# A two-layer decoder trunk in split float32: one 256-column product for the norms' factors, and byte distances between the operands of each product stage

## The chip, the core and the metric

The kernel runs on one core of a Trainium2 chip. The metric is the device time of one execution in microseconds (us). Before the change three runs gave 594.59, 595.46 and 595.98 us; their median is 595.46 us. Beside these runs there is one profiled execution, from which every row of a trace in this document comes.

## The reference

256 tokens of width 1024 pass through two layers. Layer A has differential attention over 256 tokens, layer B has block-sparse attention, which for 256 tokens is one causal block. Both layers also attend into a fixed memory of 256 rows, and both end in a squared-ReLU MLP of width 4096.

```python
h = _rmsnorm(x, a_norm_attn[i]);  z = h @ a_w_in[i]              # 1024 x 2560
o_self = _diff_attention(q, k, v, lam, lam_init, a_subln[i])
o_mem = _memory_attention(qm, mem, a_mem_norm[i], a_w_mem_kv[i])
x = x + jnp.concatenate([o_self, o_mem], axis=-1) @ a_w_out[i]   # 1024 x 1024
u = jax.nn.relu(_rmsnorm(x, a_norm_mlp[i]) @ a_w_up[i])          # 1024 x 4096
x = x + (u * u) @ a_w_down[i]                                    # 4096 x 1024
...
hk = _rmsnorm(x, kv_norm);  kv = hk @ w_kv                       # 1024 x 1536
h = _rmsnorm(x, b_norm_attn[j]);  z = h @ b_w_in[j]              # 1024 x 1024
...
return _rmsnorm(x, final_norm)
```

## The kernel before

**Split products.** Every large product is made from three products in float32r: each operand is split into a high part (h: the value cast to float32r, by ScalarE) and a low part (l: the remainder, by VectorE), and TensorE adds h·h, h·l and l·h into one PSUM bank. Weights arrive in 192 chunks of 128 x 1024 float32 (buffers `w`), are cast into `wh` (L336) and their remainders into `wl` (L338). Names of a row read `out<-moving,stationary`: the first operand streams through the array, the second was loaded into it (PEld) beforehand, while the matmul ahead of it ran.

**The product stages,** in the order of a layer:

- `nat_block` (L497): the attention's input products. The tokens are stationary (128 columns), 512 columns of weights move. Which token tile is used depends on the call: `xn` in layer A and for keys and values in layer B, `B2`/`B3` (printed as `B`) for queries in layer B, weight buffers for the memory.
- `out_proj` (L763): weights stationary, 256 tokens of the tile pair `B0`/`B1` (the attention's output `O`) move.
- `up_chunk` (L819): weights stationary, 256 tokens of `xn` move. The first 256-column result can be used once the norms' factors are known.
- `natural_down` (L869): the tokens' activations u (`B0` to `B7`) stationary, 512 columns of weights move. For six pairs of chunks (`FAST`, `fast_pair`) seven block products take the place of eight; four of the seven have sums of blocks of u as stationary operand. These sums are split into `xn` as well (L918 on ScalarE, L919 on VectorE), two of its eight slots for each pair, four pairs before a slot is used again.

**The norms' factors.** Gains go into the tokens ahead of a product and the factor 1/rms behind it. For the MLP, `Stats.rstd` (L458) sums squares on TensorE, VectorE computes the two columns of factors (128 tokens each), and `bcast` (L475 to L479) spreads them over all partitions: two diagonal matrices of 128 x 128 on VectorE, two plain float32 products with a matrix of ones on TensorE, which the trace shows as four passes, and a copy into `rb`.

**Order.** `Plan` orders all steps by a planner with costs and priorities and emits one stream for each engine; a step waits for the last writer of what it reads and for all readers of what it overwrites, by the keys it names. Tiles of the pool `const` lie one behind the other in the order of their first use, then those of the pool `ring`; a tile starts at a multiple of 32 bytes.

**Distances.** For what follows, the distance of two successive matmuls is the byte address (within a partition) of the second one's stationary operand less that of the first one's moving operand, modulo 512; 512 bytes are the 128 float32 columns of a stationary operand. All `w`, `wh`, `wl` and `B` buffers start 416 bytes past a multiple of 512, `xn` starts 352 past one, and every step within them is a multiple of 512. So the distance is 0 in L763, in L869 with u and in L497 with `B` or the memory; 448 in L497 and L869 with `xn` as stationary operand; and 64 in L819, where `xn` moves.

Of the kernel before, what the change touches and what calls it, by code (L numbers as in the profile page):

```python
# [9 lines left out]
F32 = mybir.dt.float32  # L10
F32R = mybir.dt.float32r
# [3 lines left out]
OP = mybir.AluOpType  # L15
AX = mybir.AxisListType

D, S, FF = 1024, 256, 4096
KT = D // 128
# [5 lines left out]
HELD = 6  # L25
FAST = (1, 3, 5, 7, 9, 11)
CW = 1024

# [182 lines left out]
def t_dve(n, scalar=False):  # L213
    return 69 + 1.041 * n + (61 if scalar else 0)
# [11 lines left out]
def tile_hybrid(ctx: ExitStack, tc: tile.TileContext, xa, xb, memt, xnat, mnat, w0, wall, consts, fgain, out):  # L226
    nc = tc.nc
    const = ctx.enter_context(tc.tile_pool(name="const", bufs=1))
# [11 lines left out]
    def name(s):  # L240
        uid[0] += 1
        return f"{s}_{uid[0]}"

    def buf(cls, shape, dt=F32, pool=None):
        pool = pool or ring
        return Buf(cls, lambda slot: pool.tile(shape, dt, name=name(cls), tag=f"{cls}{slot}", bufs=1))
# [8 lines left out]
    def ppx_buf():  # L255
        return Buf("ppa", lambda slot: ppx[:, slot])

    def fixed(shape, nm, dt=F32):
        return const.tile(shape, dt, name=name(nm))


    NG = len(GAINS) * KT
    xg = fixed([128, NG + KT * S], "xT")
    xT = xg[:, NG:].rearrange("p (k s) -> p k s", k=KT)
    xnt = fixed([128, KT, 2, S], "xn", F32R)
    g = {n: xg[:, i * KT:(i + 1) * KT] for i, n in enumerate(GAINS)}
    cst = fixed([128, 513], "consts")
    trig_t = cst[:, 0:256].rearrange("p (a b e) -> p a b e", a=2, b=2)
# [8 lines left out]
    mv = fixed([128, 2, 4, 64], "mv")  # L277
    vb = fixed([128, 2, 12, 64], "vb")

    wsum = fixed([128, 2048], "wsum")  # L280


# [5 lines left out]
    ones = fixed([128, 128], "ones")  # L288
# [62 lines left out]
    def split_scaled(src, skey, gain, T, k, psrc=False):  # L351
        P.add(("act", t_act(S, psrc, True), lambda: nc.scalar.activation(T.h(k), src(), AF.Copy, scale=gain)),  # L352
              skey, [T.hk(k)])
        P.add(("dve", t_dve(S, True), lambda: nc.vector.scalar_tensor_tensor(  # L354
            T.l(k), src(), gain, T.h(k).bitcast(F32), op0=OP.mult, op1=OP.subtract)),
            list(skey) + [T.hk(k)], [T.lk(k)], port=not psrc)

    xn = Tiles(lambda k: xnt[:, k, 0], lambda k: xnt[:, k, 1], lambda k: ("xnh", k), lambda k: ("xnl", k))

    def big(i, shape, dt=F32):  # L360
        return buf(f"B{i}", shape, dt)

    def big_tiles(i, j):
        h, l = big(i, [128, KT, S], F32R), big(j, [128, KT, S], F32R)
        return Tiles(lambda k: h.t[:, k], lambda k: l.t[:, k], lambda k: (h, k), lambda k: (l, k))

    @early("prep")
    def norm_tile(gname, T, k):
# [101 lines left out]
    def bcast(st):  # L470

        ps = bank("t")
        for h in range(2):
            dg = buf("dg", [128, 128])
            P.add(("dve", 196, lambda dg=dg, h=h: nc.vector.tensor_scalar_mul(dg.t, ident, st.r[:, h:h + 1])),  # L475
                  [st.key], [dg])
            P.add(("pe", 213, lambda dg=dg, h=h: nc.tensor.matmul(
                ps.t[:, h * 128:(h + 1) * 128], ones, dg.t, start=True, stop=True)), [dg], [ps])
        P.add(("dve", t_dve(S), lambda: nc.vector.tensor_copy(rb_t, ps.t[:, 0:S])), [ps], ["rb"])  # L479


# [367 lines left out]
    def natural_down(us, pss, upto, held, gather, room, rk, depth):  # L849
# [30 lines left out]
        def fast_pair(n, j):  # L880
# [31 lines left out]
            split(3, lambda: t(2, 4), rk(2) + rk(3))  # L912

            q = 2 * (n % depth)
            sh, sl = [xnt[:, q + i].rearrange("p a s -> p (a s)") for i in range(2)]
            kh, kl = [[("xnh", q + i), ("xnl", q + i)] for i in range(2)]
            src, sk = st_["sums"][j]
            P.add(("act", t_act(512), lambda: nc.scalar.copy(sh, src())), sk, kh)  # L918
            P.add(("dve", t_dve(512), lambda: nc.vector.tensor_sub(sl, src(), sh.bitcast(F32))), sk + kh, kl, port=True)  # L919
# [188 lines left out]
    class Mixer:  # L1108


        def __init__(self, diff, rx, qT, kT):
            self.diff, self.rx, self.qT, self.kT = diff, rx, qT, kT
            self.O = big_tiles(0, 1)
            self.vv = big(4, [128, 4, 512]) if diff else None
            st_["pT"] = big(5, [128, 5, 384]) if diff else None
            st_["pp"] = None if diff else big(5, [128, 4, 512])
            st_["p"] = big(6, [128, 4, 512])
            self.zz = big(7, [128, 4, 512])
# [148 lines left out]
    def x_prep(gname, T, st):  # L1267
        def done(m):
            norm_tile(gname, T, m)
            st.add(lambda: xT[:, m], [("x", m)])  # L1270
        return done
# [4 lines left out]
    for k in range(KT):  # L1276
        if k == 0:
            dma(lambda: xg[:, 0:NG + 4 * S], xa, 512 * (NG + 4 * S), w=["g"] + [("x", j) for j in range(4)], pri=-1)
        if k == 4:
            dma(lambda: xg[:, NG + 4 * S:], xb, 512 * 4 * S, w=[("x", j) for j in range(4, 8)], pri=3)  # L1280
        if k % 2 == 0:
            first_ch.append(chunk(2 if k == 0 else 1))
            P.steps[-5].pri = k - 0.5 if k else P.steps[-5].pri
        split_scaled(lambda k=k: xT[:, k], [("x", k), "g"], g["a_norm_attn"][:, k:k + 1], xn, k)
    ra.whole(xnat, 2)
    dma(lambda: cst, consts, 512 * 513, w=["trig", "lam", "sub8"])

# [17 lines left out]
        mem_evac(pss)  # L1305

    ma = Stats()
    mixer_a(Mixer(True, ra, xn, xn), mem_a, x_prep("a_norm_mlp", xn, ma), first_ch)

    st_["layer"] = "B"  # L1310

    rx = Stats()
    xq = big_tiles(2, 3)
    mlp(ma, x_prep("kv_norm", xn, rx))

    def mem_b():
        T = mem_tiles("b_mem_norm")
# [3 lines left out]
        rx.rstd()  # L1321

    mb = Stats()
    mixer_b(Mixer(False, rx, xq, xn), mem_b, x_prep("b_norm_mlp", xn, mb))

    mlp_last(mb)

# [75 lines left out]
```

## Time and profile before

| what | value |
|---|---|
| median of three runs | 595.46 us (594.59 to 595.98) |
| the profiled execution: its own time, and the span of its trace | 598.83 us, 597.1 us |
| mean granted TensorE clock | 0.996 |
| matmul records | 3794 |
| DMA | 108.45 MB, 182 GB/s on average |

All starts and durations below are of the profiled execution, counted from the start of its span. Where a row of the chain says that x matmuls took so many us, the quotient is the time from one matmul's start to the next, which will be called the pitch; the duration of a single record is longer, since matmuls overlap. The same quotient can be formed from two rows of the timeline: the difference of their starts by the matmuls between them.

### The profile page before, as it was taken

How to read it: one execution, taken by the hardware profiler on the slowest of the kernel's cores; microseconds unless marked ns; L12 is line 12 of the kernel's file. 1: busy time of each engine (PE TensorE's matmuls, PEld its weight loads, DVE VectorE, ACT ScalarE, POOL GpSimd, SP SyncE). 2: the span in 40 equal slices, each digit the busy share in tenths (PEclk: the TensorE clock that was granted, in tenths of full speed). 3: DMA queues.
4: the chain of work that ended last, by engine and by line, in shares of the span. 5: the costliest groups of instructions: out<-in, count | busy, mean ns of one | idle time of the engine just before them, and what ended most of it. 6: DMA issues, size and time to landing. Idle time of an engine off the chain costs nothing.

```text
span 597.1 us, 10365 instructions
## 1 busy us (share of the span) xinstructions
PE 586.0 (98%) x3794; PEld 517.7 (87%) x3794; DVE 485.2 (81%) x869; ACT 390.1 (65%) x749; POOL 56.1 (9%) x67
## 2 busy tenths in 40 slices
PE   8999999999999999999999999999999999999995
PEld 7777878999999988888888887889999999888884
DVE  6699886789877898988988688786886767998874
ACT  6788797666665575555786588776575565665632
POOL 0131020240000000000122131001300000000002
PEclk9999999999999999999999999999999999999998
DMA  8974715336656536567576633334565555356531
GB/s 302 343 259 137 257 65 167 118 122 228 207 182 209 181 111 224 193 209 247 173 232 233 211 125 124 106 93 159 183 205 199 188 178 177 141 177 245 180 104 71
DMA packets 30003, 108.45 MB, mean 182 GB/s; under 512 B 3328, under 2 KB 3328, under 8 KB 29696
## 3 DMA queue, kind: packets, MB, share of 16 engines
q1 hardware_dynamic: 29664, 107.26, 53.5%
q8 instruction: 30, 0.49, 0.3%
q10 hardware_dynamic: 288, 0.52, 0.2%
q14 instruction: 21, 0.17, 0.1%
HBM read 106.72 MB, written 1.05 MB: 181 GB/s over the span
## 4 chain that ended last, share of the span: by engine, by line
PE 88%; DMA 4%; DVE 4%; ACT 3%; issue 1%; SPq 0%; DVEq 0%; ACTq 0%
PE acc L819 30%; PE t L869 22%; PE acc L497 16%; PE acc L763 7%; PE acc L869 6%; DMA w<-wall 2%; PE t L584 2%; PE t L622 2%; PE t L679 1%; DVE wl L338 1%; DMA w<-memt 1%; ACT wh L336 1%; PE t L555 1%; DMA xT<-xa 1%; DVE xT L749 0%
## 5 line engine op out<-in xcount | busy, mean ns | idle before, releaser
L336 ACT CAST wh<-w 128x512 fp32r<-128x512 f32 (+1 forms) x232 | 182.4, 816 | 119.8 <-PE acc L819 44.5
L338 DVE TENSOR_TENSOR wl<-w,wh 128x512 fp32r<-128x512 f32 (+1 forms) x232 | 213.8, 943 | 32.6 <-ACT wh L336 32.0
L819 PE MATMUL acc<-xn,wh 128*128 128x256 f32 x1024 | 130.2, 279 | 1.1 <-DVE xn L354 1.1
L819 PEld LDWEIGHTS acc<-xn,wh 128*128 128x128 f32 x1024 | 123.4, 188 | 1.5 <-DVE xn L354 1.3
L869 PE MATMUL t<-wh,B 128*128 128x512 f32 (+1 forms) x368 | 111.9, 386 | 0.0
L497 PE MATMUL acc<-wh,xn 128*128 128x512 f32 x256 | 86.1, 404 | 0.9 <-ACT xn L352 0.9
L869 PEld LDWEIGHTS t<-wh,B 128*128 128x128 f32 x368 | 68.5, 188 | 13.8
L869 PE MATMUL t<-wl,B 128*128 128x512 f32 (+1 forms) x184 | 71.0, 386 | 0.0
L819 PE MATMUL acc<-xn,wl 128*128 128x256 f32 x512 | 70.1, 279 | 0.0
L819 PEld LDWEIGHTS acc<-xn,wl 128*128 128x128 f32 x512 | 64.0, 188 | 0.0
L497 PEld LDWEIGHTS acc<-wh,xn 128*128 128x128 f32 x256 | 48.9, 191 | 13.4 <-issue 1.4
L497 PE MATMUL acc<-wl,xn 128*128 128x512 f32 x128 | 50.9, 397 | 0.2 <-DVE wl L338 0.2
L763 PE MATMUL acc<-B,wh 128*128 128x256 f32 x256 | 50.8, 289 | 0.0
L450 POOL TENSOR_TENSOR sqa<-sqa,sq 128x256 f32<-128x256 f32 x21 | 20.3, 966 | 235.4 <-ACT sq L449 234.4
L788 DVE SCALAR_TENSOR_TENSOR u<-acc,rb 128x512 f32<-128x512 f32 x32 | 21.9, 690 | 24.6 <-PE acc L819 24.5
L763 PEld LDWEIGHTS acc<-B,wh 128*128 128x128 f32 x256 | 41.1, 191 | 0.6 <-issue 0.5
L869 PEld LDWEIGHTS t<-wl,B 128*128 128x128 f32 x184 | 34.6, 188 | 7.0
L763 PE MATMUL acc<-B,wl 128*128 128x256 f32 x128 | 36.1, 282 | 0.0
L531 POOL TENSOR_TENSOR ropet<-ropes,consts 128x256 f32<-128x256 f32 (+1 forms) x28 | 25.8, 940 | 105.1 <-ACT ropes L520 77.0
L892 ACT CAST wh<-wsum 128x1024 fp32r<-128x1024 f32 x24 | 25.3, 1052 | 8.6 <-PE acc L819 3.2
L791 ACT ACTIVATE u<-u 128x512 f32<-128x512 f32 x32 | 20.1, 632 | 16.3 <-DVE u L788 16.2
L603 ACT ACTIVATE B<-t,nm 128x128 f32<-128x128 f32 (+1 forms) x64 | 27.1, 440 | 4.6 <-DVE nm L599 2.7
(221 smaller groups left out, 853.7 us busy)
## 6 DMA issues: line engine op xcount, KB each, us to landing
w<-wall SPq DMA_DIRECT2D x191, 512.0 KB, 3.5
w<-memt SPq DMA_DIRECT2D x4, 512.0 KB, 5.1
B<-xnat SPq DMA_DIRECT2D x1, 1024.0 KB, 7.5
B<-mnat SPq DMA_DIRECT2D x1, 1024.0 KB, 9.6
xT<-xa SPq DMA_DIRECT2D x1, 540.0 KB, 4.0
w<-w SPq DMA_DIRECT2D x2, 256.0 KB, 3.5
xT<-xb SPq DMA_DIRECT2D x1, 512.0 KB, 6.8
consts<-consts SPq DMA_DIRECT2D x1, 256.5 KB, 5.1
```

The lines of the kernel that those rows point to most:

```text
L336: P.add(("act", t_act(n), lambda sl=sl: nc.scalar.copy(h.t[:, sl], w.t[:, sl])), [(w, x) for x in q], [(h, x) for x in q])
L338: P.add(("dve", t_dve(n), lambda sl=sl: nc.vector.tensor_sub(l.t[:, sl], w.t[:, sl], h.t[:, sl].bitcast(F32))), [(w, x) for x in q] + [(h, ...
L450: P.add(("pool", t_pool(S), lambda: nc.gpsimd.tensor_tensor(self.acc.t, self.acc.t, sq.t, op=OP.add)), [sq, self.acc], [self.acc])
L497: nc.tensor.matmul(pss[hf].t[:, c0:c1], a(k)[:, ts], b.t[:, o + c0:o + c1], start=(k == 0 and i == 0), stop=(k == KT - 1 and i == 2))
L531: nc.gpsimd.tensor_tensor(t.t[:, 0:nh, e:e + 32], zs.t[:, 0:nh, 32 - e:64 - e], b(sin[:, e:e + 32]), op=OP.mult)
L603: nc.scalar.activation(p[hd].t[:, c], sp[hd].t[:, c], AF.Exp, bias=nm[hd][:, qb:qb + 1], accum_out=ss[:, hd, qb:qb + 1])
L763: nc.tensor.matmul(o, a.t[:, ws], x(k), start=(n == 0 and m % 2 == 0 and i == 0), stop=(n == KT - 1 and i == 2), skip_group_check=True)
L788: P.add(("dve", t_dve(512, True), lambda u=u, ps=ps: nc.vector.scalar_tensor_tensor(u.t, ps.t.rearrange("p (a s) -> p a s", a=2), 0.0, rb_ ...
L791: P.add(("act", t_act(512), lambda u=u: nc.scalar.activation(u.t, u.t, AF.Square)), [u], [u])
L819: nc.tensor.matmul(ps.t[:, o], w.t[:, k * 128:(k + 1) * 128], xnt[:, k, x], skip_group_check=True, **flags)
L869: nc.tensor.matmul(ps.t[:, c0:c1], x, y, start=start and i == 0, stop=stop and i == 2, skip_group_check=True)
L892: P.add(("act", t_act(m), lambda: nc.scalar.copy(h[x].t[:, :m], src())), keys, [h[x]])
```

## The change

- `bcast` makes one 128 x 256 matrix (two diagonal blocks, by one VectorE multiplication of broadcast views) and one product of 256 columns with the ones. It uses a buffer of class `sq` in place of two of class `dg`.
- The tile `xn` becomes 16 float32 (64 bytes) longer, and two views of it are used: `xn` at offset 0 and `xs_` at offset 16 (`LEAD`). The MLP's tokens (L819) keep the view at 0; the attention's tokens and the sums of `fast_pair` use the view at 16. Since the low part of a sum now reaches 64 bytes into the next slot, its step also names that slot as written.
- The tiles `B0` and `B1`, when they hold the attention's output, become 128 float32 longer, and the tokens begin at float32 112 (448 bytes).
- Fixed tiles of up to 8 columns are packed into shared tiles of 64 columns (`small`), and a tile of 56 columns is laid ahead of `wsum`.

With that the distances of the transposes and of attention's small float32 products change too (`mk`, `qm`, `mv`, `vb` and `ppx` start 192 bytes past a multiple of 512 instead of 416). In the large stages the distances, as defined above, are then 0 in L497 and in L869 for every token tile, and 64 in L763 and in L819:

| stage | columns moved | before | after |
|---|---|---|---|
| L497 with `xn` | 512 | 448 | 0 |
| L497 with `B` or the memory | 512 | 0 | 0 |
| L763 | 256 | 0 | 64 |
| L819 | 256 | 64 | 64 |
| L869 with u | 512 | 0 | 0 |
| L869 with the sums in `xn` | 512 | 448 | 0 |

```diff
+LEAD = 16
...
+    small = {"n": 64}
+
     def fixed(shape, nm, dt=F32):
-        return const.tile(shape, dt, name=name(nm))
+        n = math.prod(shape[1:])
+        if n > 8:
+            return const.tile(shape, dt, name=name(nm))
+        n2 = n + n % 2
+        if small["n"] + n2 > 64:
+            small.update(n=0, t=const.tile([128, 64], F32, name=name("small")))
+        a = small["t"][:, small["n"]:small["n"] + n]
...
-    xnt = fixed([128, KT, 2, S], "xn", F32R)
+    xroom = fixed([128, KT * 2 * S + LEAD], "xn", F32R)
+    xnt, xnn = [xroom[:, a:a + KT * 2 * S].rearrange("p (k a s) -> p k a s", k=KT, a=2) for a in (0, LEAD)]
...
+    fixed([128, 56], "pad")
     wsum = fixed([128, 2048], "wsum")
...
-    def big_tiles(i, j):
-        h, l = big(i, [128, KT, S], F32R), big(j, [128, KT, S], F32R)
-        return Tiles(lambda k: h.t[:, k], lambda k: l.t[:, k], lambda k: (h, k), lambda k: (l, k))
+    def big_tiles(i, j, lead=0):
+        h, l = [big(x, [128, (128 if lead else 0) + KT * S], F32R) for x in (i, j)]
+
+        def at(x, k):
+            return x.t[:, lead + k * S:lead + k * S + S]
+        return Tiles(lambda k: at(h, k), lambda k: at(l, k), lambda k: (h, k), lambda k: (l, k))
...
         ps = bank("t")
-        for h in range(2):
-            dg = buf("dg", [128, 128])
-            P.add(("dve", 196, lambda dg=dg, h=h: nc.vector.tensor_scalar_mul(dg.t, ident, st.r[:, h:h + 1])),
-                  [st.key], [dg])
-            P.add(("pe", 213, lambda dg=dg, h=h: nc.tensor.matmul(
-                ps.t[:, h * 128:(h + 1) * 128], ones, dg.t, start=True, stop=True)), [dg], [ps])
+        dg = buf("sq", [128, S])
+        P.add(("dve", t_dve(S), lambda: nc.vector.tensor_tensor(
+            dg.t.rearrange("p (a s) -> p a s", a=2), ident[:, None, :].to_broadcast([128, 2, 128]),
+            st.r[:, :, None].to_broadcast([128, 2, 128]), op=OP.mult)), [st.key], [dg])
+        P.add(("pe", 427, lambda: nc.tensor.matmul(ps.t[:, 0:S], ones, dg.t, start=True, stop=True)), [dg], [ps])
...
-            sh, sl = [xnt[:, q + i].rearrange("p a s -> p (a s)") for i in range(2)]
+            sh, sl = [xnn[:, q + i].rearrange("p a s -> p (a s)") for i in range(2)]
             kh, kl = [[("xnh", q + i), ("xnl", q + i)] for i in range(2)]
+            kl += [("xnh", q + 2)] * (q < 6)
...
-            self.O = big_tiles(0, 1)
+            self.O = big_tiles(0, 1, 128 - LEAD)
...
-    mixer_a(Mixer(True, ra, xn, xn), mem_a, x_prep("a_norm_mlp", xn, ma), first_ch)
+    mixer_a(Mixer(True, ra, xs_, xs_), mem_a, x_prep("a_norm_mlp", xn, ma), first_ch)
...
-    mlp(ma, x_prep("kv_norm", xn, rx))
+    mlp(ma, x_prep("kv_norm", xs_, rx))
...
-    mixer_b(Mixer(False, rx, xq, xn), mem_b, x_prep("b_norm_mlp", xn, mb))
+    mixer_b(Mixer(False, rx, xq, xs_), mem_b, x_prep("b_norm_mlp", xn, mb))
```

The order of TensorE's stream is unchanged but for the broadcast. This is TensorE at the beginning of layer A's `up_chunk`, before the change (`dg` are the diagonals, `sqa` the squares):

```order
L458 MATMUL t_373_1742<-ones_15_116,sqa_351_1596 128x1 x2
L819 MATMUL acc_356_1615<-xn_2_67,wl_345_1515 128x256 x4
L819 MATMUL acc_356_1615<-xn_2_67,wh_347_1538 128x256 x16
L819 MATMUL acc_356_1615<-xn_2_67,wl_348_1546 128x256 x8
L819 MATMUL acc_357_1625<-xn_2_67,wh_350_1568 128x256 x2
L819 MATMUL acc_357_1625<-xn_2_67,wl_358_1635 128x256 x8
L477 MATMUL t_385_1813<-dg_381_1805,ones_15_116 128x128
L477 MATMUL t_385_1813<-dg_382_1807,ones_15_116 128x128
L819 MATMUL acc_357_1625<-xn_2_67,wh_355_1612 128x256 x16
```

And the same place after the change, where L475 is the old L458, L835 the old L819, and L494 the new broadcast:

```order
L475 MATMUL t_269_1638<-ones_16_117,sqa_247_1492 128x1 x2
L835 MATMUL acc_252_1511<-xn_2_67,wl_241_1411 128x256 x4
L835 MATMUL acc_252_1511<-xn_2_67,wh_243_1434 128x256 x16
L835 MATMUL acc_252_1511<-xn_2_67,wl_244_1442 128x256 x8
L835 MATMUL acc_253_1521<-xn_2_67,wh_246_1464 128x256 x2
L835 MATMUL acc_253_1521<-xn_2_67,wl_254_1531 128x256 x8
L835 MATMUL acc_253_1521<-xn_2_67,wh_251_1508 128x256 x2
L494 MATMUL t_278_1707<-sq_275_1699,ones_16_117 128x256
L835 MATMUL acc_253_1521<-xn_2_67,wh_251_1508 128x256 x14
```

Two products of 128 columns have become one of 256, two matmuls later; in layer B it stands where the two stood.

ScalarE's stream differs in where the block sums are cast into `xn`. Before the change, the last pair's sums (from `mv`) in layer A's `natural_down` are cast among the weights of the third pair:

```order
L892 CAST wh_2909<-w_2854 128x1024
L892 CAST wh_2923<-wsum_78 128x1024
L918 CAST xn_67<-mv_76 128x512
L892 CAST wh_2936<-wsum_78 128x1024
L336 CAST wh_2955<-w_2890 128x1024
```

After the change (L935 is the old L918, L908 the old L892) they are cast among the last pair's own weights:

```order
L908 CAST wh_3033<-w_2981 128x512
L908 CAST wh_3043<-w_2993 128x1024
L908 CAST wh_3057<-wsum_79 128x1024
L935 CAST xn_67<-mv_76 128x512
L908 CAST wh_3070<-wsum_79 128x1024
```

The first pair's cast stays, and those of the second to fifth pair move later by 7 to 12 instructions in the same way, in both layers; VectorE's remainders (L919, now L936) follow them. The queues of SyncE and GpSimd are unchanged.

More of the change, by code (lines that the diff above doesn't have):

```diff
@@ L256, in ppx_buf @@
         return Buf("ppa", lambda slot: ppx[:, slot])
+    small = {"n": 64}
     def fixed(shape, nm, dt=F32):
-        return const.tile(shape, dt, name=name(nm))
+        n = math.prod(shape[1:])
[5 more added lines that the diff above has]
+        a = small["t"][:, small["n"]:small["n"] + n]
+        small["n"] += n2
+        return a if len(shape) == 2 else a.rearrange("p (a b) -> p a b", a=shape[1])
     NG = len(GAINS) * KT
@@ L356, in split_scaled @@
             list(skey) + [T.hk(k)], [T.lk(k)], port=not psrc)
-    xn = Tiles(lambda k: xnt[:, k, 0], lambda k: xnt[:, k, 1], lambda k: ("xnh", k), lambda k: ("xnl", k))
+    xn, xs_ = [Tiles(lambda k, x=x: x[:, k, 0], lambda k, x=x: x[:, k, 1], lambda k: ("xnh", k), lambda k: ("xnl", k))
+               for x in (xnt, xnn)]
     def big(i, shape, dt=F32):
         return buf(f"B{i}", shape, dt)
-    def big_tiles(i, j):
-        h, l = big(i, [128, KT, S], F32R), big(j, [128, KT, S], F32R)
-        return Tiles(lambda k: h.t[:, k], lambda k: l.t[:, k], lambda k: (h, k), lambda k: (l, k))
+    def big_tiles(i, j, lead=0):
[3 more added lines that the diff above has]
+        return Tiles(lambda k: at(h, k), lambda k: at(l, k), lambda k: (h, k), lambda k: (l, k))
     @early("prep")
@@ L1283, in tile_hybrid @@
             P.steps[-5].pri = k - 0.5 if k else P.steps[-5].pri
-        split_scaled(lambda k=k: xT[:, k], [("x", k), "g"], g["a_norm_attn"][:, k:k + 1], xn, k)
+        split_scaled(lambda k=k: xT[:, k], [("x", k), "g"], g["a_norm_attn"][:, k:k + 1], xs_, k)
     ra.whole(xnat, 2)
```

## The prediction

> **What bounds the kernel.** I read the page's busy times first, then the chain of work that ended last, then TensorE's waits, and then the timeline of TensorE alone, for the pitch of its matmuls.
>
> ```profile
> PE 586.0 (98%) x3794; PEld 517.7 (87%) x3794; DVE 485.2 (81%) x869; ACT 390.1 (65%) x749; POOL 56.1 (9%) x67
> ...
> PE 88%; DMA 4%; DVE 4%; ACT 3%; issue 1%; SPq 0%; DVEq 0%; ACTq 0%
> ```
> ```profile
> PE acc L819 <- DVE xn L354: 1.1, 1, 1.1
> ```
>
> TensorE carries 88% of the chain, and its longest wait for another engine is 1.1 us. A busy share of 98% says little by itself, since the records overlap; but without gaps the time is the number of matmuls by their pitch, and the order of TensorE's stream is kept but for the broadcast. So the question is whether the pitch changes. The chain gives it for whole stretches:
>
> ```profile
> 116.71 5.76 PE acc L763 x48
> ...
> 140.86 73.45 PE acc L819 x648
> ...
> 242.27 2.06 PE acc L869 x9
> 244.33 6.12 PE t L869 x27
> ...
> 430.66 76.32 PE acc L819 x648
> ```
>
> The two stages that move 256 columns differ: L763 takes 5.76/48 = 120.0 ns, L819 takes 73.45/648 = 113.3 ns in layer A and 76.32/648 = 117.8 ns in layer B. Among those with 512 columns, L869 takes 6.12/27 = 226.7 ns with u and 2.06/9 = 228.9 ns with the block sums in `xn`. L497 has the same pair in layer B, 13 triples with `B` as stationary operand, and then 14 triples with `xn`:
>
> ```profile
> 322.66 0.62 PE L497 MATMUL acc<-wh,B 128*128 128x512 f32 x2
> ...
> 331.50 0.62 PE L497 MATMUL acc<-wh,B 128*128 128x512 f32 x2
> ...
> 332.87 0.62 PE L497 MATMUL acc<-wh,xn 128*128 128x512 f32 x2
> ...
> 342.48 0.62 PE L497 MATMUL acc<-wh,xn 128*128 128x512 f32 x2
> ```
>
> 8.84 us for 39 matmuls are 226.7 ns, 9.61 us for 42 are 228.8 ns. The instructions of the two halves agree in kind and shape, and none waits: what differs is the tile that is read. With 512 columns the distance 0 goes with 226.7 ns and 448 with 228.8; with 256 columns 0 goes with 120.0, and 64 with 113.3 or 117.8. The change gives each stage the distance that goes with the shorter pitch here.
>
> A rule of the Trainium skill speaks against it: "TensorE: Matmul & The Clock Gate", section "Step-by-step: what each phase is for", says that TensorE has two independent read ports and that loading the next weights takes no read bandwidth from the running matmul. By it an address could not matter and the sum below would be 0; the 2.1 ns between the halves of L497 speak against the rule, though they do not show what else those tiles might share.
>
> **The change part by part.**
>
> *L763, distance 0 to 64.* The stage has 256 + 128 = 384 matmuls, and attention's small products cut it into stretches:
>
> ```profile
> L763 PE MATMUL acc<-B,wh 128*128 128x256 f32 x256 | 50.8, 289 | 0.0
> L763 PE MATMUL acc<-B,wl 128*128 128x256 f32 x128 | 36.1, 282 | 0.0
> ```
> ```profile
> 101.96 2.88 PE acc L763 x24
> ...
> 109.80 5.04 PE acc L763 x42
> ...
> 382.08 2.15 PE acc L763 x18
> ...
> 396.82 1.43 PE acc L763 x12
> ...
> 403.51 10.26 PE acc L763 x84
> ```
>
> The stretches of 18 and more (24, 42, 48, 18 and 84: 216 matmuls) run at some 120 ns. At L819's pitches they would take 2.2 to 6.7 ns less each: 0.5 to 1.4 us, and I take the middle, 4.4 ns by 216 = 0.95 us. The short ones take 1.43/12 = 119 ns with a restart of the stream in it, so they have not settled at 120; for the other 168 matmuls I take 1 ns each, 0.15 us, between 0 and 2.2 ns (0.4 us). Together **1.1 us**, between 0.5 and 1.8. Behind the stage, in layer A, VectorE adds the residual and splits the norm's tokens before L819 can run on; that starts from the last sums of L763, so the gain passes through.
>
> *L497 with `xn`, 448 to 0.* 256 + 128 = 384 matmuls:
>
> ```profile
> L497 PE MATMUL acc<-wh,xn 128*128 128x512 f32 x256 | 86.1, 404 | 0.9 <-ACT xn L352 0.9
> L497 PE MATMUL acc<-wl,xn 128*128 128x512 f32 x128 | 50.9, 397 | 0.2 <-DVE wl L338 0.2
> ```
> ```profile
> 57.08 3.32 DMA w<-wall
> ```
>
> At 2.1 ns these are 0.8 us. But up to about 61 us the chain still passes over transfers of weights, and one call of `nat_block` is 48 matmuls: three of the eight calls with `xn` lie there, and what they gain is spent waiting. I count the other 240: **0.5 us**, between 0.4 and 0.8.
>
> *L869 with the sums in `xn`, 448 to 0.* 6 pairs by 4 sums' products of 3 matmuls by 2 layers are 144 matmuls, of which each is 2.2 ns shorter: **0.3 us**, between 0.2 and 0.3.
>
> *The sums' splits move later.* If a remainder comes too late, TensorE waits for it in the middle of `natural_down`, and behind it on VectorE stand the next chunk's remainders, for which TensorE would wait next. The last pair of layer A moves most:
>
> ```profile
> 266.49 2.35 DVE L893 TENSOR_TENSOR wl<-wsum,wh 128x1024 fp32r<-128x1024 f32 x2
> ...
> 272.10 0.62 PE L869 MATMUL t<-wh,xn 128*128 128x512 f32 x2
> ```
> ```profile
> L919 DVE TENSOR_TENSOR xn<-mv,xn x2: 683/684/685, 236.3 to 528.6; 128x512 fp32r<-128x512 f32 x2
> ```
>
> VectorE is done with that pair's weights at 268.84 now. With 0.68 us more ahead of the last of them it is done at 269.5, and TensorE first reads these sums at 272.1. So 2.6 us cover it: **0**. The slot that the step newly names belongs to the third pair, three pairs earlier on TensorE. If the cover is gone, each of the two layers pays what is missing of it.
>
> *The broadcast.* Four passes of 128 columns become two of 256, if a plain float32 product of 256 columns is made in two passes like the others:
>
> ```profile
> 140.42 0.44 PE t L477 x4
> ```
> ```profile
> L679 PE MATMUL t<-B,vb 128*64 128x256 f32 x24 | 3.9, 400 | 0.0
> L679 PE MATMUL t<-B,vb 128*64 128x128 f32 x24 | 2.3, 272 | 0.0
> ```
>
> A pass takes 110 ns now. Nothing in the trace shows a plain float32 pass of 256 columns on the full array. From above, 128 more columns cost 128 ns (400 - 272, L679): two passes of 238 are 476 ns, 0.04 us more than now. From below, a pass at L819's 113 ns: 227 ns, 0.21 us less. L679 is also plain float32, so I take its end, rounded: **0**, with -0.4 to +0.1 us for both layers. The one multiplication on VectorE replaces two, and TensorE goes on with L819 while it runs.
>
> *L819, distance 64 as before.* Its pitch isn't fixed by the distance: 113.3 and 117.8 both stand at 64. The timeline shows where it turns (the start of a group to that of the next, by its count):
>
> ```profile
> 136.25 2.05 PE L819 MATMUL acc<-xn,wh 128*128 128x256 f32 x16
> 138.14 1.10 PE L819 MATMUL acc<-xn,wl 128*128 128x256 f32 x8
> ```
> ```profile
> 421.77 1.81 PE L819 MATMUL acc<-xn,wh 128*128 128x256 f32 x14
> 423.42 1.10 PE L819 MATMUL acc<-xn,wl 128*128 128x256 f32 x8
> ...
> 425.97 1.98 PE L819 MATMUL acc<-xn,wh 128*128 128x256 f32 x16
> 427.79 1.07 PE L819 MATMUL acc<-xn,wl 128*128 128x256 f32 x8
> ```
>
> In layer A it is 1.89/16 = 118 ns between the squares' sum (L458) and the broadcast, and 113.3 behind the broadcast. In layer B it is 1.65/14 = 118 ns ahead of the sum, 1.82/16 = 114 between the two and 117.8 behind. So each insertion that I can read (three) turns the pitch, and it then stays through 648 matmuls. A stretch that changes costs or brings 76.32 - 73.45 = 2.9 us, more than all else here. If the new broadcast still turns it, both long stretches stay as they are; if it doesn't, one gains what the other loses, as long as the stage is entered as now. In both cases I take **0**.
>
> **The sum.** 1.1 + 0.5 + 0.3 = 1.9 us. From the profiled execution's own 598.83 us that gives 596.9. It lies 3.4 us above the median of the runs, and the same difference from the median gives 595.46 - 1.9 = **593.6 us**. With the terms' ends (0.5 + 0.4 + 0.2 - 0.1 = 1.0, and 1.8 + 0.8 + 0.3 + 0.4 = 3.3) this case reaches from 592.2 to 594.5.
>
> **The rivals.**
>
> *A long stretch of L819 changes to the short pitch.* L763 now has L819's distance, so the stage may be entered in another way, and a broadcast of 256 columns may lead into it differently. Then layer B's stretch takes 2.9 us less: 590.7 us. Against it: nothing in the trace says which way an entry goes.
>
> *A long stretch changes to the long pitch.* The same mechanism at the same place, with the opposite sign: layer A's stretch goes from 113.3 to 117.8 ns behind its broadcast. That is +2.9 - 1.9 = +1.0 us, 596.5 us, and slower it is from the point at which the distances bring less than 2.9 us. If the runs, which lie 3.4 us below the profiled execution, already have the short pitch in both layers, both can be lost: +5.7 - 1.9, 599.3 us.
>
> *The distances do nothing.* The pitch of L763 and of L497 with `xn` would then hang on something else than the distance, as the order of their operands (L763 alternates two moving tiles, L819 doesn't in its `wl` half). For it: one kernel shows one tile for each distance. Against it: L497 and L869 differ by the same 2.1 to 2.2 ns with the same tile. Then it is 595.4 us.
>
> **How the numbers follow.** Forecast 0.45, one stretch shorter 0.22, one longer 0.15, both longer 0.05, distances do nothing 0.13. What a measurement of this kernel can tell from no change is about 0.2%, 1.2 us. Faster by more are the first two but for the upper edge of the forecast: 0.65. Within it are that edge, the distances that do nothing and two thirds of one longer stretch: 0.25. Slower: 0.10. The range leaves out both stretches longer and the outer edges: from 590.7 less 0.9 to 596.5 plus 0.5, 589.8 to 597.0; the forecast's own is 592.2 to 594.5.
>
> **What would show it.** Right: L763's long stretches at 113 to 118 ns, L497 with `xn` and L869 with the sums at 226.7 ns from beginning to end, and L819's two long stretches at 73.4 and 76.3 us in either order. Wrong: L763 still at 120, or `xn` as stationary operand still at 229; a wait of TensorE for L919's step in `natural_down`; and, for the total, two equal long stretches of L819.

## The result, and the profile after

Six runs of the changed kernel gave 601.18 to 602.69 us, median 601.47; six runs of the kernel before beside them gave 594.59 to 598.80 us, median 595.92. The ratio estimated from these runs is 1.0074, with a 95% interval of 1.0053 to 1.0096 (the two medians by themselves give 1.0093): **slower by 0.7%**, where 593.6 us and a range of 589.8 to 597.0 were forecast. The profiled execution of the changed kernel took 601.18 us (span 599.4 us, granted clock 0.996).

TensorE carries as much of the chain as before, where it had 88%:

```profile
PE 89%; DVE 4%; DMA 4%; ACT 2%; issue 1%; SPq 0%; DVEq 0%; ACTq 0%
```

These are the rows of the chain that answer to those shown of before (start, duration, line, matmuls; L779 was L763, L835 was L819, L885 was L869, L513 was L497):

```profile
64.20 2.96 PE acc L513 x12
...
103.28 2.74 PE acc L779 x24
...
111.04 4.78 PE acc L779 x42
...
117.67 5.67 PE acc L779 x48
...
136.68 4.82 PE acc L835 x40
141.93 76.08 PE acc L835 x646
...
245.92 2.04 PE acc L885 x9
247.96 6.12 PE t L885 x27
...
385.41 2.07 PE acc L779 x18
...
406.55 9.74 PE acc L779 x84
...
433.19 76.32 PE acc L835 x648
```

Three things are to be seen. The pitch of L779 fell: 4.78/42 = 113.8 ns where 5.04/42 = 120.0 stood, 9.74/84 = 116.0 for 122.1. The block sums of L885 now run like u, 2.04/9 = 226.7 ns for 228.9. And layer A's long stretch of the up product rose from 113.3 to 76.08/646 = 117.8 ns, so that **both** long stretches have the long pitch. The timeline shows the input product with `xn`, which ran at 228.8 ns before:

```profile
338.42 0.61 PE L513 MATMUL acc<-wh,xn 128*128 128x512 f32 x2
...
346.58 0.39 PE L513 MATMUL acc<-wh,xn 128*128 128x512 f32 x1
```

8.16 us for 36 matmuls are 226.7 ns. From here on, 117.8 ns is called the long pitch and 113.3 ns the short one.

To compare kernels without the scatter of their start, I use the row "acc x12" of the input product, which starts at 63 to 66 us, behind the wait for the first transfers. In the kernel before it is

```profile
62.87 2.96 PE acc L497 x12
```

From its start to the end of the span the kernel before took 597.1 - 62.87 = 534.23 us, the changed one 599.4 - 64.20 = 535.20 us. So of the 2.3 us between the two spans 1.0 lies behind that place and 1.3 ahead of it.

### The profile page after: what moved, and what is told of

Its sections match the earlier page's. It is cut to its first block, busy times and chain, and to the rows that moved or that the text cites. A ratio compares the mean times of both kernels' runs of the same rounds, so it can differ in the third digit from the quotient of the medians.

```text
span 599.4 us, 10359 instructions
## 1 busy us (share of the span) xinstructions
PE 585.6 (98%) x3790; PEld 517.4 (86%) x3790; DVE 485.8 (81%) x867; ACT 390.2 (65%) x749; POOL 56.2 (9%) x67
## 4 chain that ended last, share of the span: by engine, by line
PE 89%; DVE 4%; DMA 4%; ACT 2%; issue 1%; SPq 0%; DVEq 0%; ACTq 0%
PE acc L835 30%; PE t L885 22%; PE acc L513 16%; PE acc L779 7%; PE acc L885 6%; PE t L600 2%; DMA B<-mnat 2%; PE t L638 2%; PE t L695 1%; DMA w<-wall 1%; DVE wl L351 1%; PE t L571 1%; DMA xT<-xa 1%; DVE xT L765 0%; ACT wh L349 0%
## 5 line engine op out<-in xcount | busy, mean ns | idle before, releaser
L835 PE MATMUL acc<-xn,wh 128*128 128x256 f32 x1024 | 132.5, 282 | 1.1 <-DVE xn L367 1.1
L835 PEld LDWEIGHTS acc<-xn,wh 128*128 128x128 f32 x1024 | 125.4, 189 | 1.7 <-DVE xn L367 1.5
L885 PE MATMUL t<-wh,B 128*128 128x512 f32 (+1 forms) x368 | 111.9, 386 | 0.0
L513 PE MATMUL acc<-wh,xn 128*128 128x512 f32 x256 | 84.7, 398 | 2.4 <-ACT wh L349 1.7
L885 PEld LDWEIGHTS t<-wh,B 128*128 128x128 f32 x368 | 68.6, 188 | 13.8
L835 PE MATMUL acc<-xn,wl 128*128 128x256 f32 x512 | 71.1, 281 | 0.0
L885 PE MATMUL t<-wl,B 128*128 128x512 f32 (+1 forms) x184 | 71.0, 386 | 0.0
L835 PEld LDWEIGHTS acc<-xn,wl 128*128 128x128 f32 x512 | 64.9, 189 | 0.0
L513 PEld LDWEIGHTS acc<-wh,xn 128*128 128x128 f32 x256 | 48.0, 188 | 14.5 <-ACT wh L349 2.1
L513 PE MATMUL acc<-wl,xn 128*128 128x512 f32 x128 | 50.2, 392 | 0.3 <-DVE wl L351 0.2
L779 PE MATMUL acc<-B,wh 128*128 128x256 f32 x256 | 49.3, 285 | 0.0
L779 PEld LDWEIGHTS acc<-B,wh 128*128 128x128 f32 x256 | 40.4, 189 | 0.6 <-issue 0.5
L885 PEld LDWEIGHTS t<-wl,B 128*128 128x128 f32 x184 | 34.5, 188 | 6.9
L779 PE MATMUL acc<-B,wl 128*128 128x256 f32 x128 | 35.6, 278 | 0.0
L908 ACT CAST wh<-wsum 128x1024 fp32r<-128x1024 f32 x24 | 25.3, 1052 | 7.7 <-PE acc L835 3.4
L619 ACT ACTIVATE B<-t,small 128x128 f32<-128x128 f32 (+1 forms) x64 | 27.2, 440 | 4.6 <-DVE small L615 2.7
```

The costliest lines, as they stand in the source:

```text
L513: nc.tensor.matmul(pss[hf].t[:, c0:c1], a(k)[:, ts], b.t[:, o + c0:o + c1], start=(k == 0 and i == 0), stop=(k == KT - 1 and i == 2))
L619: nc.scalar.activation(p[hd].t[:, c], sp[hd].t[:, c], AF.Exp, bias=nm[hd][:, qb:qb + 1], accum_out=ss[:, hd, qb:qb + 1])
L779: nc.tensor.matmul(o, a.t[:, ws], x(k), start=(n == 0 and m % 2 == 0 and i == 0), stop=(n == KT - 1 and i == 2), skip_group_check=True)
L835: nc.tensor.matmul(ps.t[:, o], w.t[:, k * 128:(k + 1) * 128], xnt[:, k, x], skip_group_check=True, **flags)
L885: nc.tensor.matmul(ps.t[:, c0:c1], x, y, start=start and i == 0, stop=stop and i == 2, skip_group_check=True)
L908: P.add(("act", t_act(m), lambda: nc.scalar.copy(h[x].t[:, :m], src())), keys, [h[x]])
```

## The experiments

**Theory 1:** the form of the broadcast decides into which pitch the up product goes on. **Theory 2 (rival):** the layout and the way into the stage decide it. The first four runs take the change apart.

*e0_before.* The kernel before, unchanged.

> The kernel before, unchanged, for a second profile. Theory 1 (the form of the broadcast decides): both long stretches of the MLP's up product start behind a broadcast of two 128-column products; the timed runs near 595.5 us then have 113.3 ns in both layers, those near 598.5 us 117.8 ns in one. So if this profile's own time is near 595.5, both stretches show 113.3 ns; if near 598.5, one of them 117.8. Theory 2 (layout and the way the stage is entered decide): the same stretches as in the first profile, 113.3 and 117.8, whatever the time. The start: if the 1.35 us by which the changed kernel was later at 62 us is a matter of this kernel's addresses, this profile reaches that place at 61.6 us again; if it is the transfers' chance, it differs by 1 us or so.

Ten runs, median 596.40 us, ratio to the kernel before 0.9998 (0.9983 to 1.0014). The profiled execution took 596.96 us, between the two times that the expectation named.

```profile
63.71 2.97 PE acc L497 x12
...
136.70 4.58 PE acc L819 x38
141.72 73.45 PE acc L819 x648
...
426.40 4.82 PE acc L819 x40
...
431.66 73.46 PE acc L819 x648
```

Here both long stretches are short, where the first profile of the same kernel had 76.32 us in layer B. Theory 2 in its plain form falls: one program does both. The row of 40 matmuls between the squares' sum and the broadcast in layer B has the long pitch here. From the row at 63.71 to the end it is 531.49 us, 2.74 less than in the first profile, where the one stretch has 2.86 more. The start is 0.8 us later than in the first profile, in the same kernel.

*e1_two_products.* The changed kernel with two products of 128 columns.

```diff
-        P.add(("pe", 427, lambda: nc.tensor.matmul(ps.t[:, 0:S], ones, dg.t, start=True, stop=True)), [dg], [ps])
+        for h in range(2):
+            P.add(("pe", 213, lambda h=h: nc.tensor.matmul(
+                ps.t[:, h * 128:(h + 1) * 128], ones, dg.t[:, h * 128:(h + 1) * 128], start=True, stop=True)), [dg], [ps])
```

> The changed kernel, but the broadcast on TensorE is two 128-column products from the one diagonal matrix. Theory 1: both long stretches go back to 113.3 ns; 601.5 - 2 x 2.9 = 595.7 us, and the address distances show as gains against the kernel before only as far as the start does not take them back. Theory 2: both stretches stay at 117.8 ns, 601.5 us.

Ten runs, median 595.33 us (593.73 to 598.14), ratio 0.9975 (0.9960 to 0.9991). This one line makes 5 to 6 us; the order of every engine's instructions is otherwise that of the changed kernel. In its profile (597.30 us) one long stretch is short and one long:

```profile
135.56 4.82 PE acc L837 x40
140.82 73.23 PE acc L837 x646
...
424.21 4.65 PE acc L837 x40
429.31 76.32 PE acc L837 x648
```

In both layers the pitch turns at the broadcast: 4.82 us for 40 matmuls is the long pitch, 4.65 the short one (a restart of 0.1 us is in both rows), and the long stretch has the other. Theory 1 as it was put, with both stretches short, misses layer B: the form of the broadcast acts on the pitch ahead of it, and that pitch counts too.

*e2_one_product.* The kernel before with only the new broadcast. The class `dg` gets one buffer of 256 columns in place of two of 128.

```diff
-        for h in range(2):
-            dg = buf("dg", [128, 128])
...
+        dg = buf("dg", [128, S])
...
+        P.add(("pe", 427, lambda: nc.tensor.matmul(ps.t[:, 0:S], ones, dg.t, start=True, stop=True)), [dg], [ps])
```

> The kernel before with only the new broadcast: one 256-column product. Theory 1: both long stretches run at 117.8 ns in every run; 595.5 + 2 x 2.9 = 601.3 us, and no distance changes: L763 at 120.0 ns, the input product with xn at 229 ns. Theory 2: 595.5 to 598.5 us as before.

Four runs, median 603.84 us, ratio 1.0119 (1.0096 to 1.0142). Both long stretches are long:

```profile
143.79 76.08 PE acc L818 x646
...
436.19 76.32 PE acc L818 x648
```

The broadcast alone does it, without any new distance. Of the 2.5 us above the expectation, 1.0 is behind the row at 64.38 (538.22 us against 531.49 + 2 x 2.87): attention uses `dg` too (L730), and with one buffer its steps stand in another order. The rest is of the size by which the start scatters (below).

*e3_o_lead_undone.* The changed kernel with the attention's output back at byte 0.

```diff
-            self.O = big_tiles(0, 1, 128 - LEAD)
+            self.O = big_tiles(0, 1)
```

> The changed kernel with the attention's output back at byte 0 of its tiles, so that the output product has distance 0 again. Both theories of the distances' worth: its matmuls go from 115.4 back to 119.5 ns, +1.5 us. Theory 2 (the way into the up product decides the pitch): in addition at least one long stretch turns to 113.3 ns, 601.5 + 1.5 - 2.9 = 600.1 us or below. Theory 1: both stay at 117.8, 603.0 us.

Four runs, median 602.10 us (600.78 to 602.45). Both long stretches stay long, 76.08 and 76.32 us. From the row at 63.63 to the end it is 536.47 us, 1.27 more than in the changed kernel. That is what L779's distance is worth, where 1.5 were expected; the row of 84 matmuls of this stage takes 10.26 us again, as before the change.

**Which property of the broadcast?** The number of passes (one matmul record of the trace each: four before, two now) or their width (128 or 256 columns)?

*f1_one128* has one product of 128 columns and leaves out the factors of the second 128 tokens, *f2_three128* has three products:

```diff
+            for x, n in [(0, 128), (128, 128), (0, 128)]:
+                nc.tensor.matmul(ps.t[:, x:x + n], ones, dg.t[:, x:x + n], start=True, stop=True)
```

> The changed kernel with one 128-column product in the broadcast, two passes of 128 columns; the factors of the second 128 tokens are left out and the first ones stand in their place. If the number of passes decides (four turn the pitch, two do not), the long stretches keep the pitch that the stretch ahead of the broadcast has, or end at 117.8 ns as with two passes of 256 columns: 601.3 us. If the width of a pass decides, they turn as with two products: 117.8 ahead gives 113.3 behind, 595.6 us with both turned.

> The changed kernel with three 128-column products, six passes; the third makes the first half again. If the number of passes decides with a period of four, this is as two passes, 117.8 ns behind 117.8, 601.8 us; if the width of the passes decides, it turns the pitch, 113.3 behind 117.8, 596.1 us.

One run each: 593.86 and 595.86 us. In both kernels both long stretches are short (73.23 and 73.47 us), from either pitch ahead. f1:

```profile
135.59 4.65 PE acc L840 x40
140.46 73.23 PE acc L840 x646
...
423.58 4.82 PE acc L840 x40
428.62 73.47 PE acc L840 x648
```

So the number of passes does not decide: two passes of 128 columns lead to short where two of 256 led to long.

**Other distances.** *s1_distances*, *s2_distances* and *s3_distances* shift the views of `xn` and of the attention's output, with the two-product broadcast:

```diff
-    xnt, xnn = [xroom[:, a:a + KT * 2 * S].rearrange("p (k a s) -> p k a s", k=KT, a=2) for a in (0, LEAD)]
+    xua, xub, xna, xnb, xnn = [xroom[:, a:a + KT * 2 * S].rearrange("p (k a s) -> p k a s", k=KT, a=2) for a in (40, 8, 24, 40, 8)]
...
-            self.O = big_tiles(0, 1, 128 - LEAD)
+            self.O = big_tiles(0, 1, 80 if diff else 48)
```

> The changed kernel with two 128-column products in the broadcast and other distances, each in one stage of one layer: up product 128 (layer A) and 256 (B), output product 192 (A) and 320 (B), input product with the attention's tokens 320 (A) and 384 (B), block sums 256. If a distance of 0 is the special case with 256 columns, all four run between 113 and 118 ns; if 64 is the special case, they run at 120. With 512 columns: if 0 is the special case, all run at 229 ns; if what counts is how far the two addresses lie apart, 256 differs from 384 and 320. A distance that beats 113.3 or 226.7 ns would be worth more than the whole change: 1.5 us for each ns in the up product.

> As the run before with up product 192 (layer A) and 384 (B), output product 32 (A) and 448 (B), input product 64 (A) and 128 (B), block sums 32. Same alternatives: 113 to 118 ns where only 0 is special with 256 columns, 229 ns where only 0 is special with 512; a distance of 32 shows whether the special case is exactly 0 or a window around it.

> The changed kernel with two 128-column products in the broadcast and finer distances: up product 96 (layer A) and 80 (B), output product 48 (A) and 112 (B), input product 8 (A) and 224 (B), block sums 240. The runs so far read alike at distances that differ by 256, and 64 has the shortest pitch with 256 columns. If the pitch falls off steadily on both sides of it, 80 lies below 118.7 (128) and 96 between; a pitch under 113.3 ns at 80 or 96, or under 226.7 ns at 240, would be a better place for the tiles.

One run each: 604.28, 604.23 and 604.02 us, all some 3 to 4 us above the changed kernel. The table gives the mean time from one start to the next, without waits (137 to 225 matmuls for each distance with 512 columns, 566 at 0; some 645 with 256):

| distance | 0 | 8 | 32 | 64 | 80 | 96 | 128 | 192 | 224 | 240 | 256 | 320 | 384 | 448 |
|---|---|---|---|---|---|---|---|---|---|---|---|---|---|---|
| 512 columns, ns | 226.7 | 230.6 | 233.1 | 233.3 | | | 232.3 | | 233.3 | 226.7 | 226.7 | 233.3 | 232.4 | 228.9 |
| 256 columns, up product, ns | | | | 113.3 or 117.8 | 119.3 | 117.3 | 118.7 | 117.8 | | | 120.0 | | 118.7 | |

In s1, for example, the up product took 76.67 us for 646 matmuls at 128 and 77.75 us for 648 at 256. Distances that differ by 256 read alike in the three pairs that there are (0 and 256, 64 and 320, 128 and 384). The output product agrees: its row of 42 matmuls took 4.77 us at 192, 4.96 at 32 and 5.00 at 48, where the changed kernel has 4.78 at 64; its row of 84 took 9.74 us at 320, 10.10 at 448 and 10.17 at 112, where the changed kernel has 9.74. So of those tried, the change has none but the best: no distance beats 226.7 or 113.3 ns, and in the up product only 64 held a short pitch through a long stretch, though each of the others had one stretch only.

At distance 0 at least, it is the distance and not the place of one operand alone: by the sizes of the fixed tiles, the buffers of the weights and of u lie 224, 128 and 32 bytes further on (modulo 512) in s1, s2 and s3 than in the changed kernel, and the products with u, at distance 0, keep their 226.7 ns (6.12 us for 27) in all of them.

**Many products in one run.** *h1_probes* puts products of ones into the up product, in front of every second chunk, into a PSUM bank that nobody reads:

```diff
+            for n in probe if k == 0 else ():
+                nc.tensor.matmul(pb.t[:, 0:n], ones, cst[:, 0:n], start=True, stop=True, skip_group_check=True)
```

> The changed kernel with a product of ones into an unread bank ahead of every second chunk of the up product from its ninth on; what they compute is left out of the output. In layer A one of 128 columns (twice), of 256 (twice), two of 128 (twice), 128, 256, 128, two of 128 (twice), 256. In layer B 128, 64, 256, 64, 192, 256, 192, 512, 128, 512, 128 and two of 1 column. Rule from the runs so far: behind one product of 128 columns the pitch is 113.3, behind one of 256 it is 117.8, whatever it was ahead, and two of 128 turn it. So layer A reads short, short, long, long, short, long, short, long, short, long, short, long. If it is chance, the twelve stretches do not follow this. The sizes 64, 192 and 512 have no forecast.

One run, 610.31 us with the added products. Nine of the twelve stretches of layer A came as forecast, which is not enough for a rule. A row of 48 matmuls takes 5.45 us at the short pitch and 5.66 at the long one; these are the first, second, fourth and eighth, behind the first and second product of 128 columns and the second and third of 256:

```profile
152.23 5.66 PE acc L841 x48
158.10 5.47 PE acc L841 x48
...
170.09 5.65 PE acc L841 x48
...
194.06 5.45 PE acc L841 x48
```

In all four cases the pitch ahead of the product was long. The first 128 let it stand, the second turned it; the second 256 let it stand, the third turned it. Theory 1 in the form "the width decides" falls: something else counts too, and the place is what the next run varies.

*h2_places* varies the place by single matmuls (`probe` is the position in a chunk and the number of columns):

```diff
+                if 2 * k + x == probe[0]:
+                    nc.tensor.matmul(pb.t[:, 0:probe[1]], ones, cst[:, 0:probe[1]], start=True, stop=True, skip_group_check=True)
```

> The changed kernel with 24 products of ones into an unread bank within the up product, each one matmul or more further on or back than a multiple of 48 from the last; what they compute is left out of the output. Layer A: twelve of 256 columns, with 48, 49, 50, 51, 52, 53, 48, 47, 46, 45 and 44 matmuls between them. Layer B: 256 and 128 in turn, the 128s 48, 49, 51, 54, 58 and 53 matmuls behind the 256s. Theory a (the width decides): every stretch behind a 256 has 117.8 ns, every one behind a 128 has 113.3. Theory b (the place decides too): from 113.3 ns a 256 always leads to 117.8 and a 128 never does, but from 117.8 ns both can end either way, as the number of matmuls since the last interruption falls; then at least one 256 in layer A leads to 113.3, and at least one 128 in layer B to 117.8.

One run, 609.40 us with the added products. Theory b holds, by which the outcome from the long pitch changes with the place. Layer A, where each row but the first two starts behind a probe of 256 columns:

```profile
137.51 4.82 PE acc L839 x40
142.76 8.24 PE acc L839 x70
151.44 5.45 PE acc L839 x48
157.32 5.77 PE acc L839 x49
163.52 5.89 PE acc L839 x50
169.84 6.01 PE acc L839 x51
176.29 5.91 PE acc L839 x52
182.62 6.24 PE acc L839 x53
189.30 5.45 PE acc L839 x48
```

5.45/48 and 5.91/52 are 113.5 and 113.7 ns, short; 5.77/49, 5.89/50, 6.01/51 and 6.24/53 are 117.7 to 117.8, long. Behind 70, 51 and 53 matmuls of long pitch the same product led to short, behind 40, 49 and 50 to long; from short it always led to long. The table counts four kinds of product that stand in the up product at distance 64, in the 15 profiles that have it. The squares' sum, in the last line, is the kernels' own:

| put in | from short to short / long | from long to short / long |
|---|---|---|
| one product of 128 columns | 11 / 0 | 6 / 6 |
| one product of 256 columns | 0 / 13 | 8 / 19 |
| two of 128, side by side | 0 / 4 | 6 / 0 |
| the squares' sum | 0 / 18 | 10 / 2 |

Of the other kinds there are one or two each: from short, f2's three products of 128 columns left short, while h1's products of 192 and 512 columns and its two of one column led to long.

The pitch ahead, the product and the place are not all of it. In the kernel before, the squares' sum of layer B stands behind a row of 70 matmuls of 8.53 us in both profiles. In the second profile it led from long to long (the row of 4.82 us in e0), in the first, at the same place, from long to short:

```profile
425.57 4.65 PE acc L819 x40
```

**The change's own place.** *i1_one_later* and *i2_two_later* put the changed kernel's broadcast one and two matmuls later; otherwise the order of every engine's instructions stays that of the changed kernel:

```diff
             for x in range(2):
                 mm(k, wh, x, start=mi == k == x == 0, stop=False)
+                if bc and at == 2 * k + x:
+                    spread(*bc)
```

> The changed kernel with its one 256-column broadcast one matmul later in both layers, 41 matmuls behind the squares' sum instead of 40; nothing else moves. The place theory: from 117.8 ns one place in three leads to 113.3. In the probes it was the one with a remainder of 2 when the stretch at 117.8 ns had been entered from 113.3 (47 and 53 led to short; 45, 48 and 49 to long), and the changed kernel's 40 has the remainder 1. If an entry by the squares' sum counts like one by a product of 256 columns, 41 leads to short in both layers: 600.4 - 5.7 = 594.7 us. The width theory: both stay long, 600.4.

> As the run before, two matmuls later: 42 behind the sum. The place theory: if 41 is short, 42 is long in both layers, 600.4 us; if the entry by the sum counts otherwise, it is 42 that is short and 41 long. The width theory: long both times.

The kernel before took 598.54 us beside them (29 runs, 595.34 to 602.64). One later, twelve runs: median 600.55 us (599.83 to 601.46), ratio 1.0042 (1.0016 to 1.0067), long in both layers. Layer B has the long pitch ahead:

```profile
428.23 4.94 PE acc L847 x41
...
433.59 76.20 PE acc L847 x647
```

Two later, twelve runs: median 595.00 us, ratio 0.9964 (0.9936 to 0.9992), in two groups, seven runs from 593.53 to 595.01 and five from 597.76 to 598.66. Its profile (598.54 us) is of the second group; the first has none:

```profile
136.83 5.05 PE acc L847 x42
142.32 73.00 PE acc L847 x644
...
425.47 4.87 PE acc L847 x42
430.77 76.08 PE acc L847 x646
```

At this place the product turns the pitch, from long (5.05 for 42) to short and from short (4.87) to long. My guess that 41 would be the place was wrong, the rival's 42 right. So at the broadcast itself, with nothing else moved, one matmul more changes the outcome from long; the profiles show it once for each place, and the times of twelve runs each fit it.

**A version that is meant not to depend on the place.** From short, one product of 128 columns has always left short. *g1_apart* makes the broadcast in two such products that stand some twenty matmuls apart; the second matrix waits for the copy of the first half.

```diff
+        for h in range(2):
+            dg, o = buf("sq", [128, S]), slice(h * 128, h * 128 + 128)
+            P.add(("dve", 196, lambda dg=dg, h=h: nc.vector.tensor_scalar_mul(dg.t[:, 0:128], ident, st.r[:, h:h + 1])),
+                  [st.key] + ["rb"] * h, [dg])
+            P.add(("pe", 213, lambda dg=dg, o=o: nc.tensor.matmul(ps.t[:, o], ones, dg.t[:, 0:128], start=True, stop=True)),
+                  [dg], [ps])
+            P.add(("dve", t_dve(128), lambda o=o: nc.vector.tensor_copy(rb_t[:, o], ps.t[:, o])), [ps], ["rb"])
```

> The changed kernel with the broadcast in two products of 128 columns that stand apart on TensorE (the second factor's matrix is made when the first half has been copied). By the rule (a single product of 128 columns leaves 113.3 ns) both long stretches are at 113.3 in every run: 601.5 - 5.7 = 595.8 us at most, and 594 if the changed kernel's later start was the transfers' chance. If two products turn the pitch even when they stand apart, some runs have one long stretch at 117.8 and the time spreads by 2.9 us, as with two products side by side (median 595.3).

> The version with the two products apart once more, on the same chip as the two runs before, for its time beside theirs and for a second profile: both long stretches at 113.3 ns again, 594.9 us. Against the kernel with the product one matmul later it has two more interruptions in each layer; if both have short stretches, they differ by 0.5 us at most.

Twelve runs each: medians 594.93 and 594.91 us (593.09 to 597.29, 593.19 to 596.43), ratios to the kernel before 0.9970 (0.9951 to 0.9989) and 0.9940 (0.9917 to 0.9963). The second profile:

```profile
136.68 4.42 PE acc L836 x38
141.32 2.74 PE acc L836 x24
144.28 70.74 PE acc L836 x624
...
424.93 4.82 PE acc L836 x40
429.97 2.30 PE acc L836 x20
432.48 71.19 PE acc L836 x628
```

The long stretches are short in both layers, with short ahead in A (4.42 us for 38, where e0 had 4.58 at the long pitch) and long ahead in B. Of the versions that compute all of the output and ran more than once, it has the lowest medians, but e1 (595.33) and i2 (595.00) are too near for the intervals to tell them apart. That one product of 128 columns can also leave a long pitch long (6 of 12 in the table) remains a risk: where the pitch ahead is long, this version has two chances to turn it and no guarantee.

*after_again.* The changed kernel itself, once more.

> The changed kernel itself once more, for its time beside the others and a second profile. Both long stretches at 117.8 ns again by the rule. If its later start (1.35 us at 62 us) belongs to the change, the second profile has it too; if it is the transfers' chance, the place moves by about a us.

Nine runs, median 600.41 us (599.46 to 601.55), ratio 1.0056 (1.0032 to 1.0080). Both stretches are long again, and the start is 1.3 us earlier than in the first profile of the same program:

```profile
62.90 2.97 PE acc L513 x12
...
140.62 76.08 PE acc L835 x646
...
431.87 76.32 PE acc L835 x648
```

598.1 - 62.90 = 535.20 us from that row to the end, the same as in the first profile. So the later start does not belong to the change: it scatters between executions of one program, and over all eighteen profiles this row starts between 62.87 and 65.97 us.

| kernel | long stretches A, B | from the row at 63 us to the end |
|---|---|---|
| before, first profile | short, long | 534.23 |
| before, second profile | short, short | 531.49 |
| changed, both profiles | long, long | 535.20 |
| changed, two products side by side | short, long | 532.41 |
| changed, product two later | short, long | 532.38 |
| changed, two products apart | short, short | 529.60 and 529.63 |

## Why the prediction was wrong

*L763's distance: right.* The stretches named took 26.09 us; now 2.74 + 4.78 + 5.67 + 2.07 + 9.74 = 25.00 us, 1.1 less for 0.95 forecast. Undone by itself, the distance costs 1.27 us behind 63 us (1.1 forecast for the whole stage).

*L497 and L869 with `xn`: right.* Both run at 226.7 ns. Together the distances bring 531.49 + 2 x 2.87 - 535.20 = 2.0 us behind 63 us, for 1.9 forecast. Against this stood a rule of the Trainium skill ("TensorE: Matmul & The Clock Gate", section "Step-by-step: what each phase is for"): two read ports, so that loading the next weights takes no read bandwidth from the running matmul. What the prediction drew from it, that an address cannot matter, does not hold here: the same tiles of the input product run at 226.7 ns at distance 0 and at 233.3 at 64, and the measurement decides.

*The sums' splits: right.* No wait of TensorE for L936 appears among its waits.

*The broadcast's own cost: right.* From the end of the x40 row (136.68 + 4.82 = 141.50) to 141.93 it is 0.43 us, for 0.44 before.

*The net of L819: wrong, and most of the miss.* The step said that if the new broadcast does not turn the pitch, "one gains what the other loses", and took 0 in both cases. Two things failed in it. First, it took the profiled execution's pair, one short and one long, for the kernel's state; but the forecast was laid on the median of the runs, which lies 3.4 us below that execution, and e0, whose time is 1.9 us below that execution, shows both short. From there the change could only lose. Second, it took the broadcast as something that turns the pitch or leaves it, with the stage's entry deciding the rest. Two products of 128 columns side by side turned it in 10 of 10 cases (six broadcasts and four pairs added in h1), so with the old broadcast the result hung on the pitch ahead, which differs from run to run; the new one, at 40 matmuls behind the squares' sum, led to long from short (2 of 2) and from long (10 of 10), in every kernel that has it there. Two stretches at 2.9 us are the 5.7 us; less 2.0 that is 3.7 us, as the table says (531.49 to 535.20).

The rival with both stretches long had this price, 599.3 us, and named the condition (the runs lie 3.4 us below the profile), but it got a chance of 0.05 and was left out of the range. The 3.4 us were the clue, one stretch and a bit, and should have been followed. Beside *after_again* the kernel before took 596.67 us, 3.74 less than the changed one's 600.41, as these 3.7 us say; the rest of the miss is there that the base of 595.46 us, a median of three runs, lay 1.2 us low. In the first comparison the difference was 5.55 us; the other 1.8 are of the size of the start's scatter, and were not settled further.

*What stays open:* what the state is that one matmul more or less changes, and that differs between two executions of one program at the same place. The runs show that it is there, that equal products can end in either pitch, and that from short the outcome went by the kind of product in every case counted. They don't show a mechanism.

## What to carry to other kernels

Where a stage of equal matmuls can run at two pitches, look at each stretch in several profiles of the same program before laying a forecast on a median: runs that differ by the price of one stretch can mean that the profile at hand is one of several cases. When a small product is put into such a stage, or its place or form is changed, its own duration is the least of it; the pitch it leaves behind is multiplied by all that follow. The address distance between the running matmul's moving operand and the next stationary one is worth a sweep: here it is worth up to 3% of a stage with 512 columns (226.7 to 233.3 ns) and 6% with 256 (113.3 to 120.0).

## What the runs showed of the hardware

- A matmul's pitch here depends on the distance between the two operands' addresses, alike in the three pairs of distances 256 bytes apart: with 512 columns 226.7 ns at 0, 240 and 256, up to 233.3 elsewhere; with 256 columns 120.0 at 0 and 256, 113.3 or 117.8 at 64.
- At distance 64 with 256 columns both pitches hold for hundreds of matmuls, until another product comes between. That is probably also why the runs of the kernel before spread so far, from 594.59 to 602.64 us over all of them, where the changed kernel, long in both profiles, spreads from 599.46 to 602.69; only two of the runs before have a profile.
- A plain float32 product of 256 columns stands in the trace as two matmul records (four of L494 for two products), 0.43 us together.

```profile
L494 PE MATMUL t<-sq,ones x4: 377/377/377, 141.3 to 432.8; 128*128 128x256 f32 x4
```
